# A hybrid Hyena and attention layer on one core: filter taps made with time on partitions, and the bias added by a DMA

## The chip, the cores and the metric

The kernel runs on one core of a Trainium2 chip. The metric is the device time of one execution in microseconds (us). Before the change the median of three runs is 2493.93 us (2493.28 to 2494.87). The core has TensorE (PE, matmuls; PEld are its weight loads), VectorE (DVE), ScalarE (ACT), GpSimd (POOL) and SyncE (SP), each with an instruction queue of its own that runs in order, and 16 DMA engines.

## The reference

One encoder layer on x of 1 x 512 x 2048, all in float32. The part that the change touches is the Hyena branch (1024 channels): a long two-sided filter for each channel, made by a small network from positions, is applied by FFT to z, and a bias per channel times z is added.

```python
def implicit_filter(L, w1, b1, w2, b2, w3, b3, w4, freq):
    ...
    h = jnp.sin(fr * (h @ w3.astype(f32) + b3.astype(f32)))
    h = h @ w4.astype(f32)
    ...
    decay = jnp.exp(-t[:, None] * deltas[None, :])
    h_fwd = h[:, :HYENA_W] * decay
    h_bwd = h[:, HYENA_W:] * decay
    k = jnp.concatenate([h_fwd, jnp.zeros((1, HYENA_W), f32), h_bwd[:0:-1]], axis=0)
    return k / jnp.sum(jnp.abs(k), axis=0, keepdims=True)

def hybrid_layer(x, ...):
    proj = rms_norm(x, mix_norm_g) @ w_in
    u_h, q, k, v, g = jnp.split(proj, [c0, c1, c2, c3], axis=-1)
    x0, x1, hv = jnp.split(centred_short_conv(u_h, hy_conv_w, hy_conv_b), HYENA_ORDER + 1, axis=-1)
    filt = implicit_filter(S, ...)
    z = hv * x1
    z = bidir_fft_conv(z, filt) + hy_bias * z
    y_h = z * x0
    ...                                    # attention on q, k, v gives y_a
    merged = g_h * (y_h @ w_br_hyena) + g_a * (y_a @ w_br_attn)
    x = x + merged @ w_out
    ...                                    # then a SwiGLU feed-forward
```

## The kernel before, in words

Activations lie with channels on partitions and the 512 tokens along the row; a tile is 128 x 512. Every product in full precision is split: a float32 operand becomes a rounded high part and a low rest (`split`: a cast on ScalarE, a subtraction on VectorE), and `mm3` multiplies high by high, high by low and low by high. Weights come as tiles of eight 128 x 128 blocks (`wblk`, lines 180 to 198): one DMA on SyncE, one cast `wh` on ScalarE, one subtraction `wl` on VectorE, three buffers each.

The main stream of TensorE is a row of column groups (`group`): the inputs x1, hv and x0 of the Hyena branch in order of channel tiles (`px`, `phv`), the keys and values (`kv`), the queries (`q`) and gates, and so on. After every block, three matmuls, it calls `step()`. A queue of Python generators runs behind `step()`: each `yield n` puts the rest of that work n steps later. So TensorE's order is written out by the program, and the numbers in `TURN_WAIT`, `Y_WAIT` and the yields are distances in steps. A scheduler places the other engines' work around it when the program is built. `flush()` behind `kv` runs what is left.

The Hyena channels are worked in four quarters q of two tiles c. For each quarter:

- `taps_gen(q)` (line 372): the last filter layer. For each tile, two products `fp` of 128 channels by 512 positions, forward and backward half, with the columns of `w4s` as weights and the hidden activations `hh` and `hl` as moving data; times the decay `dec` (lines 381 to 387). ScalarE sums |taps| along the row (`scr`, lines 391, 392), VectorE turns that into the norm `rn`, adds norm times bias to the tap at zero (line 395), and folds the two halves into sum `hs` and difference `hd` (lines 403 to 406).
- `filter_gen(q)` (line 411): sixteen 128 x 128 transposes `ktp` in two groups of eight bring time onto partitions (lines 417 to 422); ScalarE and VectorE turn them by cos and sin (`kt`, lines 426, 427) and split them. `TURN_WAIT` steps later come the spectrum products `kp`, VectorE makes `G` and `K` of them, and GpSimd stores `K` to DRAM (`kd`).
- `conv_gen(q)` (line 467): transposes of the folded input (`ztp`), eight steps on the products `up`, times the spectrum read back (`kc`), giving `Y`; then `taps_gen(q + 1)`, and `Y_WAIT` steps later the inverse products `ab`, scaled by `rn` into `abs_`; last the `y` rows (lines 533 to 543), multiplied by the gate input x0.

Work tiles of the filter come from the tag `wk` with seven buffers, scratch from `tmp` with five.

Of the kernel before, what the change touches and what calls it, by code (L numbers as in the profile page):

```python
# [118 lines left out]
def layer_kernel(tc, wpk, xT, par, flt, zemb, w4, decT, tb2, rope, qkg, out):  # L119
# [251 lines left out]

    def taps_gen(q):

        w4s = w4t.pop(q)
        rn, hs_l, hd_l = [], [], []
        for c in range(2):
            dec = cw(f"dec{q}{c}", [P, S], "dec", 1)
            nc.scalar.dma_start(dec, decT[2 * q + c])
            fd = work(f"fd{q}{c}")
            bd = cw(f"bd{q}{c}", [P, S + 1], "bd", 1)  # L380
            for half, dst in ((0, fd), (1, bd[:, :S])):
                fp = ps_tile(f"fp{q}{c}{half}")
                csl = slice(half * 256 + c * P, half * 256 + (c + 1) * P)
                mm(fp, w4s[:, csl], mlp["h"][0], True, False)
                mm(fp, w4s[:, csl], mlp["h"][1], False, True)
                nc.vector.tensor_tensor(dst, fp, dec, ALU.mult)
                yield 2
            nc.vector.memset(bd[:, S:S + 1], 0.0)
            n2 = cw(f"n2{q}{c}", [P, 2], "n2", 3)
            scr = tmp(f"scr{q}{c}")  # L390
            nc.scalar.activation(scr, fd, AF.Abs, accum_out=n2[:, 0:1])
            nc.scalar.activation(scr, bd[:, 1:], AF.Abs, accum_out=n2[:, 1:2])
            r = cw(f"rn{q}{c}", [P, 1], "rn", 4)
            nc.vector.tensor_tensor(r, n2[:, 0:1], n2[:, 1:2], ALU.add)
            nc.vector.scalar_tensor_tensor(fd[:, :1], r, pcol("hyb", 2 * q + c), fd[:, :1], ALU.mult, ALU.add)
            nc.vector.tensor_scalar(r, r, 256.0, None, ALU.mult)
            nc.vector.reciprocal(r, r)
            rn.append(r)

            hs, hd = work(f"hs{q}{c}"), work(f"hd{q}{c}")  # L400
            ahead = fd.rearrange("p (m n) -> p n m", n=2)
            back = bd[:, 1:].rearrange("p (m n) -> p n m", n=2)[:, ::-1]
            for h, op in ((hs, ALU.add), (hd, ALU.subtract)):
                h = h.rearrange("p (n m) -> p n m", n=2)
                nc.vector.tensor_tensor(h[:, :, :P], ahead[:, :, :P], back[:, :, :P], op)
                nc.vector.tensor_tensor(h[:, :, P:][:, :, ::-1], ahead[:, :, P:], back[:, :, P:], op)
            hs_l.append(hs)
            hd_l.append(hd)
        folded[q] = rn, hs_l, hd_l

    def filter_gen(q):
        rn, hs_l, hd_l = folded.pop(q)
# [3 lines left out]
        taps = []  # L416
        for i, src in enumerate((hs_l, hd_l)):
# [5 lines left out]
            with tc.high_priority():  # L423
                for j in range(2):
                    t = tmp(f"kt{q}{i}{j}")
                    nc.scalar.activation(t, tps[1 - j], AF.Copy, scale=pcol("sina" if i == j else "nsina"))
                    nc.vector.scalar_tensor_tensor(t, tps[j], pcol("cosa"), t, ALU.mult, ALU.add)
                    taps.append(split(cv, t, "kh", "kl", 4, 4, f"k{i}{q}{j}"))
            yield 3
# [1095 lines left out]
```

## Time and profile before

| | |
|---|---|
| median of 3 runs | 2493.93 us |
| profiled execution | 2493.58 us, its span 2491.8 us |
| stretch of the Hyena branch and the keys | about 60 to 375 us |
| transposes `ktp` | 64, between 89.1 and 312 us |
| tap products `fp` | 32, between 66.1 and 287 us |
| spectrum products `kp` | eight groups of six, between 100 and 326 us |
| last inverse products `ab` | end at 371 us |
| granted TensorE clock in all stretches | 1.00 |

How to read the rows. A row of a list of groups gives line, engine, operation, output and inputs by the program's names, shape and count; then the time that the group was busy, the mean ns of one, and the idle time of the engine just before them with what ended it. A row of a timeline gives start and length in us; several instructions of one kind are merged (x8). A row of one tile's instructions gives durations as min/median/max in ns. A row of waits gives the engine that waited, what it waited for, us in total, how often, and the longest. TensorE's durations overlap, since its matmuls are pipelined: the next one starts before the last one ends.

### The profile page before, as it was taken

How to read it: one execution, taken by the hardware profiler on the slowest of the kernel's cores; microseconds unless marked ns; L12 is line 12 of the kernel's file. 1: busy time of each engine (PE TensorE's matmuls, PEld its weight loads, DVE VectorE, ACT ScalarE, POOL GpSimd, SP SyncE). 2: the span in 40 equal slices, each digit the busy share in tenths (PEclk: the TensorE clock that was granted, in tenths of full speed). 3: DMA queues.
4: the chain of work that ended last, by engine and by line, in shares of the span. 5: the costliest groups of instructions: out<-in, count | busy, mean ns of one | idle time of the engine just before them, and what ended most of it. 6: DMA issues, size and time to landing. Idle time of an engine off the chain costs nothing.

```text
span 2491.8 us, 34447 instructions
## 1 busy us (share of the span) xinstructions
PE 2485.5 (100%) x13114; PEld 2140.8 (86%) x13114; DVE 2089.3 (84%) x2972; ACT 1191.4 (48%) x1778; POOL 185.0 (7%) x297
## 2 busy tenths in 40 slices
PE   9999999999999999999999999999999999999999
PEld 7888888888888888888888888888888888888888
DVE  8899986764589999555999989999999988998888
ACT  6444334654554455443544444444444455445443
POOL 0000113020000000000000000000000002001111
PEclk9999999999999999999999999999999999999999
DMA  6434443233554444644333333333333348557754
GB/s 216 132 123 131 140 144 113 70 102 119 185 177 157 148 141 152 194 163 136 121 125 117 127 117 120 127 120 127 118 119 125 121 144 221 146 146 187 193 152 110
DMA packets 113571, 350.48 MB, mean 141 GB/s; under 512 B 13987, under 2 KB 15267, under 8 KB 113181
## 3 DMA queue, kind: packets, MB, share of 16 engines
q1 hardware_dynamic: 70128, 248.02, 30.2%
q0 software_dynamic: 22832, 63.19, 9.6%
q10 hardware_dynamic: 20445, 37.07, 4.9%
q8 instruction: 103, 1.69, 0.3%
q14 instruction: 63, 0.52, 0.1%
HBM read 297.63 MB, written 54.26 MB: 141 GB/s over the span
## 4 chain that ended last, share of the span: by engine, by line
PE 96%; DVE 2%; DMA 1%; issue 0%; ACT 0%; ACTq 0%; SPq 0%; DVEq 0%; POOLq 0%
PE fx L137 19%; PE fy L137 10%; PE b L137 7%; PE o L137 7%; PE gx L137 7%; PE px L137 6%; PE d L137 5%; PE fz L137 5%; PE dx L137 4%; PE q L137 4%; PE ex L137 3%; PE gy L137 3%; PE phv L137 2%; PE ey L137 2%; PE dy L137 2%; PE kv L137 2%
## 5 line engine op out<-in xcount | busy, mean ns | idle before, releaser
L195 DVE TENSOR_TENSOR wl<-wr,wh 128x1024 fp32r<-128x1024 f32 (+1 forms) x168 | 201.2, 1198 | 110.8 <-ACT wh L194 110.6
L194 ACT CAST wh<-wr 128x1024 fp32r<-128x1024 f32 (+1 forms) x168 | 173.3, 1032 | 236.6 <-PE o L137 67.1
L919 ACT CAST fwhs<-fs 128x1024 fp32r<-128x1024 f32 x176 | 184.8, 1050 | 88.7 <-PE fz L137 73.6
L921 DVE TENSOR_TENSOR fwls<-fs,fwhs 128x1024 fp32r<-128x1024 f32 x176 | 214.3, 1218 | 4.3 <-ACT fwhs L919 4.2
L919 ACT CAST fwha<-fa 128x1024 fp32r<-128x1024 f32 x132 | 139.0, 1054 | 149.4 <-PE fx L137 83.4
L137 PE MATMUL px<-xh,wh 128*128 128x512 f32 x576 | 179.4, 393 | 0.4 <-ACT xh L559 0.3
L137 PE MATMUL fy<-fX,fwhs 128*128 128x512 f32 x704 | 175.4, 391 | 0.0
L137 PE MATMUL fx<-fX,fwhs 128*128 128x512 f32 x704 | 175.2, 391 | 0.0
L137 PE MATMUL fx<-fX,fwha 128*128 128x512 f32 x704 | 171.8, 391 | 0.0
L921 DVE TENSOR_TENSOR fwla<-fa,fwha 128x1024 fp32r<-128x1024 f32 x132 | 161.3, 1222 | 10.0 <-ACT fwha L919 9.9
L137 PE MATMUL o<-ms,wh 128*128 128x512 f32 x512 | 157.7, 389 | 0.0
L137 PEld LDWEIGHTS fx<-fX,fwha 128*128 128x128 f32 x704 | 129.3, 188 | 25.0
L137 PEld LDWEIGHTS fx<-fX,fwhs 128*128 128x128 f32 x704 | 129.2, 188 | 25.1
L137 PEld LDWEIGHTS fy<-fX,fwhs 128*128 128x128 f32 x704 | 129.2, 188 | 24.9
L137 PEld LDWEIGHTS px<-xh,wh 128*128 128x128 f32 x576 | 106.7, 188 | 23.3 <-issue 0.7
L137 PE MATMUL d<-act,wh 128*128 128x512 f32 x384 | 118.2, 389 | 0.0
L137 PEld LDWEIGHTS o<-ms,wh 128*128 128x128 f32 x512 | 96.0, 188 | 19.8
L137 PE MATMUL px<-xh,wl 128*128 128x512 f32 x288 | 112.5, 391 | 0.0
L912 DVE TENSOR_TENSOR fs<-fa,fa 128x1024 f32<-128x1024 f32 x88 | 107.0, 1217 | 1.7 <-PE o L137 1.0
L912 DVE TENSOR_TENSOR fs<-fs,fa 128x1024 f32<-128x1024 f32 x88 | 107.2, 1218 | 0.9 <-PE o L137 0.2
L137 PE MATMUL o<-ms,wl 128*128 128x512 f32 x256 | 99.6, 389 | 0.0
L137 PE MATMUL fy<-fX,fwls 128*128 128x256 f32 x704 | 98.7, 283 | 0.2 <-DVE fwls L921 0.2
(979 smaller groups left out, 5883.0 us busy)
## 6 DMA issues: line engine op xcount, KB each, us to landing
fa<-wpk SPq DMA_DIRECT2D x176, 512.0 KB, 3.6
wr<-wpk SPq DMA_DIRECT2D x162, 512.0 KB, 3.5
ga<-wpk SPq DMA_DIRECT2D x60, 512.0 KB, 3.7
da<-wpk SPq DMA_DIRECT2D x32, 512.0 KB, 3.7
ea<-wpk SPq DMA_DIRECT2D x32, 512.0 KB, 4.4
actd<-c POOLq DMA_DIRECT2D x41, 256.0 KB, 4.2
actr<-actd ACTq DMA_DIRECT2D x41, 256.0 KB, 5.1
x2d<-dt POOLq DMA_DIRECT2D x32, 256.0 KB, 5.7
```

What stands on the lines that cost most here:

```text
L137: tc.keep_in_program_order(nc.tensor.matmul(out, lhsT=lhsT, rhs=rhs, start=start, stop=stop, **kw))
L194: casts[i] = nc.scalar.copy(st["hi"][:, c], st["raw"][:, c]).ins
L195: nc.vector.tensor_tensor(st["lo"][:, c], st["raw"][:, c], st["hi"][:, c].bitcast(F32), ALU.subtract)
L912: raws["sum"] = nc.vector.tensor_tensor(t, a, b, ALU.add).ins
L919: raws["wh"] = nc.scalar.copy(hi, w).ins
L921: raws["wl"] = nc.vector.tensor_tensor(lo, w, hi.bitcast(F32), ALU.subtract).ins
```

## The change

The hidden activations become the weights of the tap products and the columns of `w4s` the moving data, so that the taps come out with time on partitions. The positions are put in an order (`zemb`) in which each product gives the even or odd taps of one half, forwards or backwards; `hh` gets two columns more for the taps past the end, and the decay table `decP` is laid out to fit. Each product group is four matmuls of 256 columns, and no transpose follows. The fold is one add and one subtraction on whole tiles. `turn_taps` does the turning by cos and sin right behind the products of the next quarter, in its own place of the queue.

The norm is a sum over partitions now: ScalarE takes |taps|, GpSimd adds the four tiles up (`fn`) and halves the row (`fo`), and two products `nr` with a column of ones, behind `ztp` (`norm_taps`), give it per channel. The bias no longer goes into the tap at zero: ScalarE scales the folded input by half the bias (`zh`), GpSimd's queue stores it to DRAM (`zd`), and a DMA adds it to `abs_`; in the last quarter it is read back (`zr`) and VectorE adds it. The `y` rows of a quarter are made behind the first half of the next quarter's spectrum (`y_rows`).

```diff
-TURN_WAIT = 8, 8, 10, 11
+TURN_WAIT = 11, 10, 11, 11
+UP_WAIT = 11, 12, 13, 13
...
-                hh, hl = cw("hh", [P, S], "hh", dt=F32R), cw("hl", [P, S], "hl", dt=F32R)
-                nc.scalar.copy(hh, a)
-                nc.vector.tensor_tensor(hl, a, hh.bitcast(F32), ALU.subtract)
+                hh, hl = (cw(n, [P, S + 2], n, dt=F32R) for n in ("hh", "hl"))
+                for o, src in ((slice(0, 385), a[:, :385]), (slice(386, 513), a[:, 385:]),
+                               (slice(385, 514, P), a[:, P:P + 1].to_broadcast([P, 2]))):
+                    nc.scalar.copy(hh[:, o], src)
+                    nc.vector.tensor_tensor(hl[:, o], src, hh[:, o].bitcast(F32), ALU.subtract)
...
+    TAPS = ((0, 129), (386, 257)), ((1, 129), (385, 257))
     def taps_gen(q):
         w4s = w4t.pop(q)
-        for c in range(2):
-            dec = cw(f"dec{q}{c}", [P, S], "dec", 1)
-            nc.scalar.dma_start(dec, decT[2 * q + c])
...
+        for j in range(2):
+            fb = []
+            for b in range(2):
+                dec = cw(f"dec{q}{j}{b}", [P, S], "dec", 2)
+                nc.scalar.dma_start(dec, decP[4 * q + 2 * j + b])
+                fp = ps_tile(f"fp{q}{j}{b}")
+                for n in range(2):
+                    a = TAPS[b][j][n]
+                    for i in range(2):
+                        mm(fp[:, n * 256:(n + 1) * 256], mlp["h"][i][:, a:a + P], w4s[:, b * 256:(b + 1) * 256],
+                           n == 0 and i == 0, n == 1 and i == 1, skip_group_check=True)
+                f = work(f"f{q}{j}{b}")
+                nc.vector.tensor_tensor(f, fp, dec, ALU.mult)
+                if j + b:
+                    t = tmp(f"fa{q}{j}{b}")
+                    nc.scalar.activation(t, f, AF.Abs)
+                    nc.gpsimd.tensor_tensor(acc, acc, t, ALU.add)
+                else:
+                    acc = work(f"fn{q}")
+                    nc.scalar.activation(acc, f, AF.Abs)
+                fb.append(f)
+                if not b:
+                    yield 2
+            f, b = fb
+            hs = work(f"hs{q}{j}")
+            nc.vector.tensor_tensor(hs, f, b, ALU.add)
+            nc.vector.tensor_tensor(f, f, b, ALU.subtract)
+            folded[q].append((hs, f))
+            yield 2
+        norms[q] = cw(f"fo{q}", [P, 256], "fo", 1)
+        nc.gpsimd.tensor_tensor(norms[q], acc[:, :256], acc[:, 256:], ALU.add)
+
+    def norm_taps(q):
+        acc = norms.pop(q)
+        nr = ps_tile(f"nr{q}")
...
+            mm(nr[:, c:c + 1], acc[:, c * P:(c + 1) * P], pcol("one"), True, True)
+        r = cw(f"rn{q}", [P, 2], "rn", 2)
+        nc.vector.tensor_scalar(r, nr[:, :2], 256.0, None, ALU.mult)
+        nc.vector.reciprocal(r, r)
+    def turn_taps(q):
+        taps = turned[q] = []
+        for i, tps in enumerate(zip(*folded.pop(q))):
+            for j in range(2):
+                t = tmp(f"kt{q}{i}{j}")
+                nc.scalar.activation(t, tps[1 - j], AF.Copy, scale=pcol("sina" if i == j else "nsina"))
+                nc.vector.scalar_tensor_tensor(t, tps[j], pcol("cosa"), t, ALU.mult, ALU.add)
+                taps.append(split(cv, t, "kh", "kl", 4, 4, f"k{i}{q}{j}"))
     def filter_gen(q):
...
-            tps = [ps_tile(f"ktp{q}{i}{j}") for j in range(2)]
-            for j, tp in enumerate(tps):
-                for n in range(4):
-                    o = n // 2 * 256 + j * P
-                    transpose(tp[:, n * P:(n + 1) * P], src[n % 2][:, o:o + P])
...
+            if q and i == 0:
+                y_rows(q - 1, sums.pop(q - 1))
     def conv_gen(q):
...
-        yield 8
+        norm_taps(q)
+        yield UP_WAIT[q]
...
             yield from taps_gen(q + 1)
-        yield Y_WAIT[q]
+            yield 5
+            turn_taps(q + 1)
+            yield Y_WAIT[q] - 5
+        else:
+            yield Y_WAIT[q]
...
+            if ph and q == NQ - 1:
+                zr = [tmp(f"zr{c}") for c in range(2)]
+                for c in range(2):
+                    nc.scalar.dma_start(zr[c], zd[c])
...
+        if q < NQ - 1:
+            for c in range(2):
+                nc.gpsimd.dma_start(abs_[c], zd[c], accum_op=ALU.add)
+            yield 1
+            sums[q] = abs_
+            return
         yield 1
+        for c in range(2):
+            nc.vector.tensor_tensor(abs_[c], abs_[c], zr[c], ALU.add)
+        y_rows(q, abs_)
...
     queue(taps_gen(0))
-    queue(pause(18))
+    queue(pause(11))
+    queue(turn_gen())
     queue(filter_gen(0))
...
-            zl.append(z)
+            zl.append(dpool.tile([P, S], F32, tag=f"zd{ct}", bufs=1, name=f"zd{ct}"))
+            zh = tmp(f"zh{ct}")
+            nc.scalar.activation(zh, zf, AF.Copy, scale=hybh[:, ct:ct + 1])
+            nc.gpsimd.dma_start(zl[c], zh)
```

What the change moves in the queues, at three places. Names carry the quarter and tile as digits and a buffer number behind the underscore; `wl13` is the low part of weight tile 13.

TensorE in quarter 0, where the first taps were transposed: before, eight `ktp` stand between two blocks of `phv2`, and eight more four blocks later.

```order
L137 MATMUL phv2_892<-xh0_127,wl14_895 128x512
L140 MATMUL ktp000_902<-ident_83,hs00_746 128x128
L140 MATMUL ktp000_902<-ident_83,hs01_792 128x128
L140 MATMUL ktp000_902<-ident_83,hs00_746 128x128
L140 MATMUL ktp000_902<-ident_83,hs01_792 128x128
L140 MATMUL ktp001_903<-ident_83,hs00_746 128x128
L140 MATMUL ktp001_903<-ident_83,hs01_792 128x128
L140 MATMUL ktp001_903<-ident_83,hs00_746 128x128
L140 MATMUL ktp001_903<-ident_83,hs01_792 128x128
L137 MATMUL phv2_892<-xh1_148,wh14_894 128x512 x2
```

In the changed program no such group exists; TensorE's only new place is behind the transposes of the input, which stand in both (here its end, with the norm's two products).

```order
L141 MATMUL ztp01_1106<-ident_83,zf0_679 128x128
L141 MATMUL ztp01_1106<-ident_83,zf1_700 128x128
L138 MATMUL nr0_1115<-prm_78,fo0_809 128x1 x2
L138 MATMUL px13_1041<-xh7_325,wh16_1043 128x512 x2
L138 MATMUL px13_1041<-xh7_325,wl16_1044 128x512
```

Gone are the sixteen transposes of a quarter; the norm's pair is what TensorE gets instead.

VectorE in quarter 0, ahead of the weight part `wl13`; before:

```order
L598 SCALAR_TENSOR_TENSOR hvo1_682<-hv1u_683,prm_78,hvo1_682 128x511
L597 SCALAR_TENSOR_TENSOR yh0_693<-x00u_694,prm_78,yh0_693 128x511
L617 TENSOR_TENSOR z1_688<-hvo1_682,x1o1_676 128x512
L598 SCALAR_TENSOR_TENSOR yh0_693<-x00u_694,prm_78,yh0_693 128x511
L621 TENSOR_TENSOR zf1_690<-z1_688 128x256 x2
L386 TENSOR_TENSOR bd00_715<-fp001_726,dec00_712 128x512
L195 TENSOR_TENSOR wl13_855<-wr13_853,wh13_854 128x1024
```

And now:

```order
L394 TENSOR_TENSOR f010_771<-fp010_766,dec010_764 128x512
L634 SCALAR_TENSOR_TENSOR x1o1_686<-x11u_687,prm_78,x1o1_686 128x511
L634 SCALAR_TENSOR_TENSOR hvo1_692<-hv1u_693,prm_78,hvo1_692 128x511
L635 SCALAR_TENSOR_TENSOR x1o1_686<-x11u_687,prm_78,x1o1_686 128x511
L635 SCALAR_TENSOR_TENSOR hvo1_692<-hv1u_693,prm_78,hvo1_692 128x511
L394 TENSOR_TENSOR f011_789<-fp011_784,dec011_782 128x512
L654 TENSOR_TENSOR z1_698<-hvo1_692,x1o1_686 128x512
L407 TENSOR_TENSOR hs01_794<-f010_771,f011_789 128x512
L658 TENSOR_TENSOR zf1_700<-z1_698 128x256 x2
L196 TENSOR_TENSOR wl13_896<-wr13_894,wh13_895 128x1024
```

All four products of the quarter (`f`) and three of the four fold operations stand ahead of `wl13` now, where two products stood before; the eviction `x00u` and the two multiplies on `yh0` have gone behind it.

VectorE at the end of the branch, from the last scaling of `ab` on; before:

```order
L531 SCALAR_TENSOR_TENSOR abs7_3436<-ab311_3474,rn31_2783,abl311_3497 128x2x128
L538 TENSOR_TENSOR y6_3500<-abs6_3435 128x2x128
L539 TENSOR_TENSOR y6_3500<-abs6_3435 128x2x128
L538 TENSOR_TENSOR y7_3504<-abs7_3436 128x2x128
L195 TENSOR_TENSOR wl58_3695<-wr58_3693,wh58_3694 128x1024
L543 TENSOR_TENSOR yh6_2936<-yh6_2936,y6_3500 128x512
```

And now:

```order
L551 SCALAR_TENSOR_TENSOR abs7_3417<-ab311_3455,rn3_3159,abl311_3485 128x2x128
L560 TENSOR_TENSOR abs6_3416<-abs6_3416,zr0_3472 128x512
L560 TENSOR_TENSOR abs7_3417<-abs7_3417,zr1_3473 128x512
L570 TENSOR_TENSOR y6_3490<-abs6_3416 128x2x128
L196 TENSOR_TENSOR wl58_3685<-wr58_3683,wh58_3684 128x1024
L571 TENSOR_TENSOR y6_3490<-abs6_3416 128x2x128
```

Two adds of the bias have come in ahead of the last `y` rows.

More of the change, by code (lines that the diff above doesn't have):

```diff
@@ L116, in weight_blocks, with layer_kernel @@
     return out
-def layer_kernel(tc, wpk, xT, par, flt, zemb, w4, decT, tb2, rope, qkg, out):
+def layer_kernel(tc, wpk, xT, par, flt, zemb, w4, decP, tb2, rope, qkg, out):
     nc = tc.nc
@@ L354, in mlp_gen @@
                 yield 6
-    filt, kd, folded = {}, {}, {}
+    kd, folded = {}, {}
     w4t = {}
@@ L370, in w4_parts @@
         w4t[q] = w4s
+    TAPS = ((0, 129), (386, 257)), ((1, 129), (385, 257))
+    norms, rns, sums, turned = {}, {}, {}, {}
     def taps_gen(q):
         w4s = w4t.pop(q)
-        rn, hs_l, hd_l = [], [], []
-        for c in range(2):
-            dec = cw(f"dec{q}{c}", [P, S], "dec", 1)
-            nc.scalar.dma_start(dec, decT[2 * q + c])
[L379 to L408, printed above, removed]
@@ L409, in taps_gen @@
-        folded[q] = rn, hs_l, hd_l
+        folded[q] = []
+        for j in range(2):
[27 more added lines that the diff above has]
+            yield 2
@@ new lines, in taps_gen @@
+        norms[q] = cw(f"fo{q}", [P, 256], "fo", 1)
[3 more added lines that the diff above has]
+        nr = ps_tile(f"nr{q}")
+        for c in range(2):
+            mm(nr[:, c:c + 1], acc[:, c * P:(c + 1) * P], pcol("one"), True, True)
+        r = cw(f"rn{q}", [P, 2], "rn", 2)
+        nc.vector.tensor_scalar(r, nr[:, :2], 256.0, None, ALU.mult)
+        nc.vector.reciprocal(r, r)
+        rns[q] = [r[:, c:c + 1] for c in range(2)]
@@ L411, in filter_gen @@
+    def turn_taps(q):
[6 more added lines that the diff above has]
+                taps.append(split(cv, t, "kh", "kl", 4, 4, f"k{i}{q}{j}"))
     def filter_gen(q):
-        rn, hs_l, hd_l = folded.pop(q)
@@ L415, in filter_gen @@
         yield 3
-        taps = []
-        for i, src in enumerate((hs_l, hd_l)):
-            tps = [ps_tile(f"ktp{q}{i}{j}") for j in range(2)]
-            for j, tp in enumerate(tps):
-                for n in range(4):
-                    o = n // 2 * 256 + j * P
-                    transpose(tp[:, n * P:(n + 1) * P], src[n % 2][:, o:o + P])
[L423 to L429, printed above, removed]
+        taps = turned.pop(q)
         if q + 1 < NQ:
@@ L539, in conv_gen, with turn_gen @@
             nc.vector.tensor_tensor(down[:, :, ::-1], a, b, ALU.subtract)
-            while ct not in x0st:
-                yield 1
             yh[ct] = x0st[ct]
             nc.vector.tensor_tensor(yh[ct], yh[ct], y, ALU.mult)
+    def turn_gen():
+        turn_taps(0)
+        yield 6
+    hybh = cw("hybh", [P, HT], "hybh")
+    nc.vector.tensor_scalar(hybh, prm[:, PC["hyb"]:PC["hyb"] + HT], 0.5, None, ALU.mult)
     xps = [ps_tile(f"px{i}") for i in range(XW)]
@@ L615, in layer_kernel @@
             hv = short_conv(p2, 16 + ct, f"hv{ct}", cw(f"hvo{ct}", [P, S], "sc", 3))
-            z = cw(f"z{ct}", [P, S], "z", 3)
+            z = cw(f"z{ct}", [P, S], "z", 2)
             nc.vector.tensor_tensor(z, hv, x1, ALU.mult)
@@ L1439, in _constants @@
     ang = (f4(2.0 * math.pi) * pos / f4(S))[:, None] * fb[None, :]
-    zemb = two_part(np.ascontiguousarray(np.concatenate([t[:, None], np.cos(ang), -np.sin(ang)], axis=-1).T, dtype=f4)).reshape(66, S)
+    zemb = two_part(np.ascontiguousarray(np.concatenate([t[:, None], np.cos(ang), -np.sin(ang)], axis=-1).T, dtype=f4))
+    order = np.concatenate([i[:257:2], i[1:256:2], i[511:256:-2], i[510:257:-2]])
+    zemb = zemb.reshape(66, S)[:, order]
     lo_d, hi_d = math.log(1e-2) / 1.5, math.log(1e-2) / 0.3
@@ L1443, in _constants @@
     dec = np.exp(-t[:, None] * deltas[None, :]).astype(f4)
-    decT = dec.T.reshape(HT, P, S)
+    p = i[:P]
+    n = np.arange(2)[:, None]
+    at = np.stack([[2 * p + n, 2 * p + 2 - n], [510 - 2 * p + n, 512 - 2 * p - n]])
+    decP = np.concatenate([dec, np.zeros((1, HW), f4)])[at].reshape(4, 2, P, NQ, 256)
+    decP = decP.transpose(3, 0, 2, 1, 4).reshape(4 * NQ, P, S)
     inv = np.power(f4(10000.0), -np.arange(0, 64, 2, dtype=f4) / f4(64)).astype(f4)
@@ L1454, in _constants @@
             rope[:, j, :, b:b + 64] = v.reshape(NTB, P, 64).transpose(1, 0, 2)
-    return tb2, cosw, sinw, cosa, sina, zemb, decT, rope
+    return tb2, cosw, sinw, cosa, sina, zemb, decP, rope
 def _arrays(inp):
@@ L1461, in _arrays @@
     assert all(v.dtype == f4 for v in a.values())
-    tb2, cosw, sinw, cosa, sina, zemb, decT, rope = _constants()
+    tb2, cosw, sinw, cosa, sina, zemb, decP, rope = _constants()
     blocks = weight_blocks()
```

8 lines of the change are left out of this document (4 added, 4 removed).

## The prediction

> **What bounds the kernel now.** I read the page's busy shares first, then TensorE's waits, then the stretch that the change touches (60 to 375 us) by engine.
>
> ```profile
> PE 2485.5 (100%) x13114; PEld 2140.8 (86%) x13114; DVE 2089.3 (84%) x2972; ACT 1191.4 (48%) x1778; POOL 185.0 (7%) x297
> PE warm L137 <- DVE wones L252: 1.1, 1, 1.1
> PE kp L137 <- DVE k121l L216: 0.5, 1, 0.5
> PE px L137 <- ACT xh L559: 0.3, 1, 0.3
> PE fy L137 <- DVE fwls L921: 0.2, 1, 0.2
> 60.00:375.00 315.00, 314.52 (x1497) 262.54 (x1496) 285.66 (x465) 133.09 (x204) 28.95 (x48) 1.00 0.42 134
> ```
>
> The four middle rows are all waits of TensorE in the whole program. In the last row (busy time of PE, PEld, DVE, ACT, POOL, then granted clock) TensorE has 0.48 us of idle time, VectorE 29.3 us. So TensorE's instruction stream sets the time, and a removed matmul is worth its issue interval, as long as nothing new makes TensorE wait. A matmul's listed duration overlaps the next one's, so I price by the distance of starts.
>
> **The transposes of the taps** go: eight groups of eight.
>
> ```profile
> L140 PE MATMUL ktp<-ident,hs 128*128 128x128 f32 x32 | 4.1, 272 | 0.0
> L140 PE MATMUL ktp<-ident,hd 128*128 128x128 f32 x32 | 4.1, 272 | 0.0
> 88.15 0.39 PE L137 MATMUL px<-xh,wh 128*128 128x512 f32 x1
> 88.38 0.39 PE L137 MATMUL px<-xh,wl 128*128 128x512 f32 x1
> 88.61 0.62 PE L137 MATMUL phv<-xh,wh 128*128 128x512 f32 x2
> ...
> 89.29 1.03 PE L140 MATMUL ktp<-ident,hs 128*128 128x128 f32 x8
> 90.08 0.71 PE L137 MATMUL phv<-xh,wh 128*128 128x512 f32 x2
> 90.62 0.40 PE L137 MATMUL phv<-xh,wl 128*128 128x512 f32 x1
> ```
>
> A 512-column matmul starts 0.23 us after the one before (88.15, 88.38, 88.61). From 89.29 to 90.62 there are eight transposes and two such matmuls: 1.33 - 0.46 = **0.87 to 0.88 us** for a group; the first matmul behind it is some 0.09 late, and that goes too. Eight groups: **-7.0 us**.
>
> **The tap products** change operands. Each of 16 groups was two 512-column matmuls and becomes four of 256 columns.
>
> ```profile
> 66.29 0.39 PE L137 MATMUL fp<-hh,w4s 128*128 128x512 f32 x1
> 66.52 0.39 PE L137 MATMUL fp<-hl,w4s 128*128 128x512 f32 x1
> 66.75 0.63 PE L137 MATMUL px<-xh,wh 128*128 128x512 f32 x2
> 1227.94 1.12 PE L137 MATMUL fy<-fX,fwls 128*128 128x256 f32 x8
> 1228.90 2.00 PE L137 MATMUL fy<-fX,fwhs 128*128 128x512 f32 x8
> ```
>
> A group took 0.46 us (66.29 to 66.75). Eight 256-column matmuls, each with its own weights, take 0.96 us (1227.94 to 1228.90), 0.12 each, so the new group takes 0.48: 16 x 0.02 = **+0.3 us**. Were each as long as its listed 0.283 us mean duration, it would be +10 us; the starts rule that out.
>
> **The column sums** `nr` are new: two 128x1 fp32 products in each quarter, behind transposes that stand there anyway. The nearest row is the token norm, four calls that the trace shows as eight instructions.
>
> ```profile
> 57.67 0.95 PE L137 MATMUL rs1ss<-prm,acc 128*128 128x1 f32 x8
> 58.48 0.71 PE L137 MATMUL px<-xh,wh 128*128 128x512 f32 x2
> ```
>
> That is 0.81 us, 0.10 an instruction. Two calls are four instructions, 0.41 us; four quarters: **+1.65 us**. Ends: 0.8 if a call is one instruction, 1.8 if each group pays the 0.09 again.
>
> **The wait at `kp`** should go.
>
> ```profile
> 250.39 0.40 PE L137 MATMUL kp<-k121h,CS 128*128 128x512 f32 x1
> 251.26 0.49 PE L137 MATMUL kp<-k121l,CS 128*128 128x512 f32 x1 [0.47 <-DVE k121l L216]
> 251.59 0.39 PE L137 MATMUL kp<-k121h,CS 128*128 128x512 f32 x1
> ```
>
> The 0.87 + 0.33 us between these starts are two intervals of 0.23 otherwise: **-0.75 us**. Today the taps are transposed 14 steps ahead of the `kp` that reads them, a step being three matmuls, 0.69 us. In the new program they are turned 22 steps ahead in quarter 0 and 29 in the others (15 to 20 us). What is late next is the products' own inputs, below.
>
> Sum: -7.0 + 0.3 + 1.65 - 0.75 = **-5.8 us**. The profiled execution took 2493.58 us (its span of 2491.8 and 1.8 around it), so 2487.8; the median of the runs shown is 0.35 above it, so **2488.1**.
>
> **What is hidden, and by what.** VectorE folds with 16 adds of 512 columns instead of 32 of 256, and drops 32 one-column operations.
>
> ```profile
> L406 DVE TENSOR_TENSOR hs<-fd,bd x8: 399/419/427, 80.8 to 304.6; 128x256 f32<-128x256 f32 x8
> L395 DVE SCALAR_TENSOR_TENSOR fd<-rn,prm,fd x8: 208/219/220, 81.1 to 305.2; 128x1 f32<-128x1 f32 x8
> L617 DVE TENSOR_TENSOR z<-hvo,x1o x8: 678/682/693, 71.3 to 308.7; 128x512 f32<-128x512 f32 x8
> ```
>
> By durations 32 x 0.42 against 16 x 0.68 is -2.5 us, the small operations up to -5, the two `zr` adds and four pairs on `rn` +2.6: VectorE's own work falls by 2 to 5 us. The turn's multiplies and casts (`kt`, `kh`, `kl`) stay as many, with SBUF sources instead of PSUM. ScalarE gains eight `zh` (0.7 us each, as `kt` is) and ten DMA issues (0.33), loses 16 accumulator reads (0.19): about +6 of its 182 idle us. GpSimd gains 14 DMAs (0.6 each) and 16 adds, in 286 idle us. All this costs nothing while TensorE's operands are ready in time.
>
> The new waits have work to hide them. `nr` waits for GpSimd's half add, and all of TensorE stands behind it; but it comes 47 steps (32 us) after the last product. On ScalarE `zh` waits for `zf`, and issues of `dec` wait for the product that frees their buffer, with weight casts behind them; ScalarE is idle for over half of the stretch. On GpSimd the bias DMA waits for `abs`; behind it stand the `kd` stores, due 15 steps later.
>
> Two places have little cover.
>
> The first is the weight split `wl13` in quarter 0. The order shows it behind five more 512-column operations, with `x00u` and two `yh` multiplies moved behind it.
>
> ```profile
> 78.97 0.68 DVE L386 TENSOR_TENSOR bd<-fp,dec 128x512 f32<-128x512 f32 x1
> 79.57 1.21 DVE L195 TENSOR_TENSOR wl<-wr,wh 128x1024 fp32r<-128x1024 f32 x1
> 83.62 0.39 PE L137 MATMUL px<-xh,wl 128*128 128x512 f32 x1
> ```
>
> At 0.60 us from start to start (78.97 to 79.57) and 0.66 a multiply, it is 5 x 0.60 - 0.60 - 2 x 0.66 = 1.1 us later. It ended at 80.78, wanted at 83.62: cover 2.84, so 1.7 us are left. ScalarE makes the first summand for GpSimd only behind `zf1`, so the first add falls behind or upon this split.
>
> The second is the end: `zr` puts two adds (1.2 us) ahead of the last `y`, and the key's tables load behind those.
>
> ```profile
> 392.07 0.42 DVE L709 TENSOR_TENSOR ko<-ko,kt 128x256 f32<-128x256 f32 x1
> 393.00 0.60 PE L140 MATMUL kT0p<-ident,ko 128*128 128x128 f32 x4
> ```
>
> Cover there is 0.5 us. But the last inverse products stand one step (0.69 us) earlier, so the `y` rows end about 0.5 us later, and GpSimd idled 1.4 us between `rpk` and `ko`. I take 0, up to 1 us. Everywhere else the split of weights had 5 us or more, and `kp`, `ztp` and with them the loads of `kc` come earlier. The bias DMA of a quarter lands some 15 steps ahead of the `y` rows that read it; DMA is at 0.42 of its time and gets some 6 MB more.
>
> **Rivals.**
>
> **Cover eaten in places** (a wait for VectorE in place of the one at `kp`). GpSimd's adds hold up VectorE.
>
> ```profile
> 44.23 1.36 POOL L344 TENSOR_TENSOR hs<-ha,hs 64x512 fp32r<-64x512 f32 x1 [1.99 <-ACT ha L343]
> 44.35 1.78 DVE L560 SCALAR_TENSOR_TENSOR xh<-xr,prm,xh 128x512 fp32r<-128x512 f32 x1
> 31.10 0.74 DVE L560 SCALAR_TENSOR_TENSOR xh<-xr,prm,xh 128x512 fp32r<-128x512 f32 x1
> ```
>
> The same multiply takes 1.78 us begun inside such an add and 0.74 alone: 1.04 lost. Three adds in a quarter lose up to 3.1 us, 1.4 more than the 1.7 left at `wl13` if all fell ahead of it; with 1 us at the end and the like elsewhere, 1 to 4 us come back: **2489 to 2492**. For it: VectorE is busy 91% of the stretch. Against it: covers of 5 us and more elsewhere.
>
> **GpSimd's adds make VectorE the bound** (the other side). The 12 adds and four half adds are 14 adds' worth. On 128 partitions an add has only these rows:
>
> ```profile
> L675 POOL TENSOR_TENSOR rpk<-rpk,gaink x8: 447/452/1439, 381.3 to 384.3; 128x128 f32<-128x128 f32 x8
> ```
>
> 512 columns are four of those: 1.8 us. If VectorE stands still through each, it loses 14 x 1.8 = 25 us. It has 29.3 idle and gains some 3, but 17 of the idle time are waits for `kc` (10.8) and for casts (6.1):
>
> ```profile
> L498 DVE TENSOR_TENSOR cu<-up,kc 128x1024 f32<-128x1024 f32 x16 | 19.5, 1219 | 10.8 <-DMA kc<-kd 10.8
> L195 DVE TENSOR_TENSOR wl<-wr,wh 128x1024 fp32r<-128x1024 f32 x47 | 57.3, 1218 | 6.1 <-ACT wh L194 6.1
> ```
>
> Then 285.7 - 3 + 25 + 17 = 325 us of VectorE stand against 315 - 6 = 309 of TensorE: 16 us more, **2504**. It decides from about 0.7 us lost per add (10 us in all); that the `kc` wait shrinks, since `kp` is earlier, and that adds meet operations with PSUM sources speak against it. The Trainium skill, page "SBUF — State Buffer", section "SBUF: two separate sides", says that VectorE and GpSimd share one port pair as an exclusive lock and that the other one "fully blocks"; the trace agrees (1.78 against 0.74), and by that rule every add that meets a two-input operation costs its whole rest.
>
> **The change does not do what it says**: 256-column products with `hh` as weights at 0.19 us, an LDWEIGHTS' duration, instead of 0.12 would cost 64 x 0.07 = 4.5 us and give 2492.6. The `fwls` rows have a fresh weight load each at 0.12, so I hold this unlikely.
>
> **How the numbers follow.** Clean sum: 0.60 (2487.5 to 2488.9). Cheap `nr`, 2487.2: 0.04. Cover eaten: 0.25. Products dearer: 0.03. VectorE the bound: 0.08. The range leaves out the last and the edges: 2487.0 to 2492.0. A measurement of this kernel tells 0.2% from no change, 5.0 us, so faster means below 2488.9: the first two cases, 0.64; eaten cover and dear products are within, 0.28; the rest slower, 0.08. The clean sum lies only 0.8 us beyond that bound.
>
> **What would show it.** No `ktp` group; `fp` groups 0.48 us from start to start; `nr` pairs 0.41; no TensorE wait at `kp`. Wrong would be: waits of TensorE for `wl` near 83 us, for `ko` near 387, or for `Yt` at `ab`; multiplies of VectorE of 1.5 us beside `fn` adds; VectorE over 95% busy in the stretch.

## The result, and the profile after

The changed kernel takes 2513.98 us (median of 4 runs, 2512.36 to 2514.43) where the kernel before took 2493.61 us beside it: ratio 1.0079, 95% interval 1.0066 to 1.0091. The prediction was 2488.1 us, 2492.0 at most. It is 20 us slower.

First the busy row of the changed kernel's page, then the window of the Hyena branch (columns as before: busy time of PE, PEld, DVE, ACT, POOL, then granted clock, DMA share, GB/s). Its span was 2512.3 us.

```profile
PE 2490.8 (99%) x13098; PEld 2142.9 (85%) x13098; DVE 2098.7 (84%) x2929; ACT 1195.1 (48%) x1772; POOL 219.7 (9%) x327
```

```profile
60.00:375.00 315.00, 301.21 (x1390) 248.83 (x1389) 275.43 (x393) 130.70 (x187) 62.87 (x78) 0.97 0.47 145
```

TensorE now has 13.8 us of idle time in the same 315 us (0.48 before), and VectorE, which was to lose 2 to 5 us of work, has 9.4 more in the whole program. The waits of TensorE in the changed kernel, longest in total first:

```profile
PE ab L138 <- DVE cu L509: 6.3, 1, 6.3
PE up L138 <- DVE zt20l L217: 2.0, 1, 2.0
PE ab L138 <- ACT Yt311h L216: 1.6, 1, 1.6
PE phv L138 <- DVE wl L196: 1.3, 1, 1.3
...
PE kv L138 <- DVE abs L551: 1.1, 1, 1.1
PE ab L138 <- DVE f L394: 0.9, 1, 0.9
```

No `kp` among them: that wait went, as the prediction had it. The largest one is in quarter 0. Around it, TensorE's timeline, and then the windows (the third number from the end is the granted clock):

```profile
149.61 0.39 PE L138 MATMUL px<-xh,wl 128*128 128x512 f32 x1
156.31 0.77 PE L138 MATMUL ab<-CS,Yt000h 128*128 128x256 f32 x2 [6.32 <-DVE cu L509]
...
160.46 1.16 PE L138 MATMUL px<-xh,wh 128*128 128x512 f32 x2
161.42 0.63 PE L138 MATMUL px<-xh,wl 128*128 128x512 f32 x1
```

```profile
140.00:149.60 9.60, 9.60 (x45) 8.00 (x45) 9.60 (x13) 2.81 (x5) 1.02 (x2) 1.00 0.55 155
149.60:156.30 6.70, 0.39 (x2) 0.02 (x1) 6.70 (x11) 1.96 (x3) 0.22 (x1) 0.80 0.42 144
156.30:163.90 7.60, 7.23 (x24) 6.28 (x25) 7.31 (x10) 1.86 (x3) 1.64 (x2) 0.50 0.34 107
```

The stall is paid twice: 6.5 us of standing, then 7.6 us at a granted clock of 0.50, worth another 3.8. VectorE was busy all through the stall (6.70 of 6.70). The clock falls a second time in quarter 2, behind the wait of `up` for `zt20l` (2.4 us between two starts, at 274.1), to 0.50 for some 7 us, worth up to 3.4:

```profile
278.70:283.00 4.30, 4.16 (x10) 3.29 (x11) 2.70 (x6) 0.81 (x1) 1.09 (x2) 0.50 0.78 263
```

Taken over 50 to 400 us, the starts of TensorE's matmuls lie 27.0 us further apart than the median of their shapes; before it was 2.2. Less the 5 us of work that TensorE no longer has, that is the 20 us.

Why VectorE was late shows first in ScalarE's timeline, 105 to 120 us, before and after:

```profile
105.01 0.59 ACT L441 COPY kc<-kp 128x512 f32<-128x512 f32 x1 [1.28 <-PE kp L137]
105.49 0.72 ACT L450 ACTIVATE kcr<-G,prm 128x512 f32<-128x512 f32 x1
```

```profile
103.10 0.59 ACT L451 COPY kc<-kp 128x512 f32<-128x512 f32 x1 [1.98 <-PE kp L138]
...
115.79 0.72 ACT L662 ACTIVATE zh<-zf,hybh 128x512 f32<-128x512 f32 x1 [3.19 <-DVE zf L658]
116.60 1.05 ACT L195 CAST wh<-wr 128x1024 fp32r<-128x1024 f32 x1
117.55 0.71 ACT L462 ACTIVATE kcr<-G,prm 128x512 f32<-128x512 f32 x1
```

`kcr`, ScalarE's part of `K`, had its inputs at 105.3, where the last `G` ended, and stands behind `zh` of the next quarter, which waits for `zf`. So it runs 12 us later than before, and with it `K`, the `kd` stores, the `kc` loads and `Y`. Second, VectorE's and GpSimd's timelines of the changed kernel in quarter 1, where a fold should take 0.68:

```profile
162.08 1.27 POOL L398 TENSOR_TENSOR fn<-fn,fa 128x512 f32<-128x512 f32 x1 [5.41 <-ACT fa L397]
165.31 3.38 POOL L398 TENSOR_TENSOR fn<-fn,fa 128x512 f32<-128x512 f32 x2 [1.96 <-ACT fa L397]
168.76 1.07 POOL L412 TENSOR_TENSOR fo<-fn 128x256 f32<-128x256 f32 x1
```

```profile
162.15 1.75 DVE L408 TENSOR_TENSOR f<-f,f 128x512 f32<-128x512 f32 x1
...
165.74 0.68 DVE L632 TENSOR_TENSOR x02u<-px,rbc 128x512 f32<-128x512 f32 x1
166.34 1.18 DVE L408 TENSOR_TENSOR f<-f,f 128x512 f32<-128x512 f32 x1
167.45 1.78 DVE L432 SCALAR_TENSOR_TENSOR kt<-hs,prm,kt 128x512 f32<-128x512 f32 x1
169.16 1.23 DVE L634 SCALAR_TENSOR_TENSOR yh<-x02u,prm,yh 128x511 f32<-128x511 f32 x1
```

Four operations of this quarter last 3.1 us longer than alone (1.07 + 0.50 + 1.04 + 0.49); `x02u`, which reads PSUM, takes its 0.68 inside an add. Over the four quarters it is 12.2 us, about half of it in the folds and 3.6 us in `kt`. Third, in quarters 1 to 3 the `y` rows stand between the two halves of the spectrum, and `kci` waits behind them (ScalarE's timeline, quarter 2):

```profile
263.34 0.72 ACT L462 ACTIVATE kcr<-G,prm 128x512 f32<-128x512 f32 x1 [1.07 <-DVE G L454]
263.97 1.04 ACT L195 CAST wh<-wr 128x1024 fp32r<-128x1024 f32 x1
268.24 0.72 ACT L463 ACTIVATE kci<-G,prm 128x512 f32<-128x512 f32 x1 [3.23 <-DVE G L454]
```

That gave three suspects: the **order** (`zh` ahead of `K`), GpSimd's **adds**, and the place of **y**.

### The profile page after: what moved, and what is told of

Same layout as the page of the kernel before. It is cut to its first block, busy times and chain, and to the rows that moved or that the text cites. A ratio compares the mean times of both kernels' runs of the same rounds, so it can differ in the third digit from the quotient of the medians.

```text
span 2512.3 us, 34460 instructions
## 1 busy us (share of the span) xinstructions
PE 2490.8 (99%) x13098; PEld 2142.9 (85%) x13098; DVE 2098.7 (84%) x2929; ACT 1195.1 (48%) x1772; POOL 219.7 (9%) x327
## 4 chain that ended last, share of the span: by engine, by line
PE 84%; DVE 1%; issue 0%; DMA 0%; ACT 0%; POOLq 0%; DVEq 0%; ACTq 0%
PE fx L138 19%; PE fy L138 10%; PE b L138 7%; PE o L138 7%; PE gx L138 7%; PE d L138 5%; PE fz L138 5%; PE dx L138 4%; PE q L138 3%; PE ex L138 3%; PE gy L138 3%; PE ey L138 2%; PE dy L138 2%; PE gz L138 2%; PE dz L138 1%; PE g L138 1%
## 5 line engine op out<-in xcount | busy, mean ns | idle before, releaser
L961 DVE TENSOR_TENSOR fwla<-fa,fwha 128x1024 fp32r<-128x1024 f32 x132 | 161.2, 1221 | 10.1 <-ACT fwha L959 10.0
```

What stands on the lines that cost most here:

```text
L961: raws["wl"] = nc.vector.tensor_tensor(lo, w, hi.bitcast(F32), ALU.subtract).ins
```

## The experiments

All are the changed kernel with the edits named, but for two that are the kernel before with something added. Times are medians; the ratio is to the kernel before, run beside them.

| run | us | ratio, 95% interval |
|---|---|---|
| changed kernel | 2514.0 | 1.0066 to 1.0091 |
| e1 bias over z | 2503.5 | 1.0025 to 1.0054 |
| e2 no bias | 2502.5 | 1.0023 to 1.0049 |
| e3 no adds | 2501.3 | 1.0021 to 1.0049 |
| e4 adds on VectorE | 2511.9 | 1.0060 to 1.0090 |
| e5 bias over z, no adds | 2493.4 | 0.9990 to 1.0008 |
| e6 bias over z, adds by DMA | 2512.6 | 1.0063 to 1.0088 |
| e7 as e6, y later | 2505.0 | 1.0032 to 1.0057 |
| e8 nr later | 2514.6 | 1.0069 to 1.0097 |
| e9 bias over z, y later | 2500.9 | 1.0015 to 1.0038 |
| e10 as e9, no adds | 2489.9 | 0.9976 to 0.9993 |
| e11 as e9, adds on VectorE | 2490.8 | 0.9978 to 0.9997 |
| e12 before, with GpSimd adds | 2503.9 | 1.0027 to 1.0052 |
| e13 before, with VectorE adds | 2502.3 | 1.0021 to 1.0042 |
| e14 as e9, adds of 16 columns | 2488.6 | 0.9965 to 0.9985 |
| e15 as e11, up later | 2491.8 | 0.9981 to 0.9999 |
| e16 bias over z, adds on VectorE | 2496.5 | 1.0003 to 1.0023 |

### The order

**e1**, the scaled bias written over `z`:

```diff
-            zh = tmp(f"zh{ct}")
-            nc.scalar.activation(zh, zf, AF.Copy, scale=hybh[:, ct:ct + 1])
-            nc.gpsimd.dma_start(zl[c], zh)
+            nc.scalar.activation(z, zf, AF.Copy, scale=hybh[:, ct:ct + 1])
+            nc.gpsimd.dma_start(zl[c], z)
```

> The changed kernel with one edit: ScalarE writes the scaled bias over z, which nothing reads any more, instead of taking one of the five tmp buffers. In the program's order the second quarter's first zh (zh2) then no longer stands ahead of kcr on ScalarE and z, zf no longer ahead of K on VectorE; all work stays. Order theory (zh2 takes its tmp buffer ahead of kcr, so K, the kd stores and the kc loads of quarter 0 start 12 us late): K back at about 106 to 113 us, no wait of TensorE of 6.3 us at ab in quarter 0 (149.6 us), and the fall of the granted clock behind it gone too: 2514 - 6 - 4 = 2504, or lower if the later quarters start with less backlog. Adds theory (GpSimd's adds hold VectorE up by 12 us, and that is the loss): the waits come elsewhere, 2510 to 2514.

Measured 2503.5, 10.5 us less, as the order theory had it. ScalarE's instructions in quarter 0 (some left out), in the changed kernel and then in e1:

```
COPY kc01<-kp010 128x512
CAST zt00h<-ztp00 128x512
ACTIVATE hvo2<-hv2u,prm 128x512
CAST zt01h<-ztp01 128x512
ACTIVATE zh2<-zf2,hybh 128x512
ACTIVATE kcr00<-G000,prm 128x512
```

```
COPY kc01<-kp010 128x512
ACTIVATE kcr00<-G000,prm 128x512
ACTIVATE kci00<-G001,prm 128x512
```

`zh` and `kcr` both draw from the five `tmp` buffers, and `zh2` comes first in the program; given another buffer for `zh`, the scheduler puts `kcr` first again. In e1's trace `kcr` runs at 107.66, not 117.55:

```profile
107.66 0.72 ACT L462 ACTIVATE kcr<-G,prm 128x512 f32<-128x512 f32 x1
```

The 6.3 us wait is gone; smaller ones came up (2.8 us for a weight split at 94 us), so half the loss stays.

**e2**, the bias left out (`zh`, `zd`, the DMA onto `abs_`, and `zr` in the last quarter):

```diff
-            nc.scalar.activation(zh, zf, AF.Copy, scale=hybh[:, ct:ct + 1])
-            nc.gpsimd.dma_start(zl[c], zh)
...
-                nc.gpsimd.dma_start(abs_[c], zd[c], accum_op=ALU.add)
...
-            nc.vector.tensor_tensor(abs_[c], abs_[c], zr[c], ALU.add)
```

> The changed kernel without the bias: no zh, no zd, no DMA added to abs, no zr adds; the filter taps as in the change, GpSimd's adds included. Order theory: quarter 0 as without zh2, and no wait for the bias DMA ahead of G in the other quarters: 2488 to 2500, most of the 20 us back. Adds theory: at least 12 of the 20 us stay, 2506 or more.

Measured 2502.5, between the two cases: 11.5 us less, no more than e1 within the spread of the runs. So of the bias it is the buffer that costs; its eight ScalarE operations and 14 DMAs on GpSimd's queue, kept in e1, cost about 1 us or nothing.

**e8**, the column sums behind the products `up` instead of ahead of them:

```diff
-        norm_taps(q)
         yield UP_WAIT[q]
...
                 yield 5
+        norm_taps(q)
         if q + 1 < NQ:
```

> The changed kernel with the column sums nr and the two operations on rn emitted behind the four spectra products of a quarter instead of behind ztp; nothing else. VectorE waited 3.5 us for nr in quarter 0 with zt00l, hvo and the weight split behind. If that wait is a cause of the loss: 2 to 4 us less than the changed kernel, 2510 to 2512. If K behind zh2 decides, the same chain ends as late: 2513 to 2515.

Measured 2514.6: nothing. VectorE's 3.5 us wait for `nr` was real, but `K` stood behind `zh2` anyway (`kcr` at 116.79).

### GpSimd's adds

**e3** leaves the adds out (the norm is then that of one tap tile's half):

```diff
-                    nc.gpsimd.tensor_tensor(acc, acc, t, ALU.add)
...
-        nc.gpsimd.tensor_tensor(norms[q], acc[:, :256], acc[:, 256:], ALU.add)
+        nc.scalar.copy(norms[q], acc[:, :256])
```

> The changed kernel without GpSimd's adds: the 12 adds of fa to fn are left out and fo is a ScalarE copy of half of fn, so the filter's norm is that of one of its tap tiles; everything else stays, K behind zh2 too. Adds theory: VectorE gets 12 us back (its operations beside the adds last 0.45 to 1.15 us longer than alone), so 2514 less 12 to 20: 2494 to 2502. Order theory: the late K of quarter 0 is kept, so its waits stay for the most part: 2506 to 2514.

Measured 2501.3: 12.7 us less, and the wait at `ab` in quarter 0 is still there (5.8 us). The time is as the adds theory had it, the kept wait as the order theory had it: neither was the whole. **e4** makes the adds on VectorE:

```diff
-                    nc.gpsimd.tensor_tensor(acc, acc, t, ALU.add)
+                    nc.vector.tensor_tensor(acc, acc, t, ALU.add)
...
-        nc.gpsimd.tensor_tensor(norms[q], acc[:, :256], acc[:, 256:], ALU.add)
+        nc.vector.tensor_tensor(norms[q], acc[:, :256], acc[:, 256:], ALU.add)
```

> The changed kernel with the 12 adds and 4 half adds on VectorE instead of GpSimd: VectorE pays 12 x 0.6 + 4 x 0.35 = 8.6 us of its own where the trace shows it losing 12.2 us beside GpSimd's adds. If only VectorE's time counts: 3 to 4 us less, 2510. If the lock between the two engines costs more than the time that the durations show: 2500 or less. Order theory: within 4 us of the changed kernel, 2510 to 2516.

Measured 2511.9, 2.1 us less: it decides nothing, since with `K` still behind `zh2` TensorE waits for VectorE at `ab` in quarter 0 all the same (5.4 us). **e12** puts the same load on the kernel before, where nothing else is wrong (and **e13** the same with `nc.vector`):

```diff
             nc.scalar.activation(scr, bd[:, 1:], AF.Abs, accum_out=n2[:, 1:2])
+            for _ in range(2):
+                nc.gpsimd.tensor_tensor(scr, scr, scr, ALU.add)
```

> The kernel before with 16 added GpSimd adds of 128x512 (two behind each tap tile's norm, doubling a scratch tile that nothing reads), four a quarter where the change has three and a half. Nothing else. Adds theory: VectorE's operations beside them last longer by some 12 us in all, of which its idle time in the stretch (29 us) hides a part; TensorE's waits and the lower clock behind them add up to 4 to 12 us: 2498 to 2506. If adds cost only a kernel that is already behind: 2493 to 2495.

Measured 2503.9, 10.3 us more, though VectorE's and ScalarE's instructions stand in the same order as before, one by one. Two rows of VectorE's timeline, in e12 beside an add begun at 80.33, and in the kernel before:

```profile
80.43 1.02 DVE L396 TENSOR_TENSOR rn<-n 128x1 f32<-128x1 f32 x1
81.70 0.99 DVE L397 SCALAR_TENSOR_TENSOR fd<-rn,prm,fd 128x1 f32<-128x1 f32 x1
```

```profile
80.70 0.15 DVE L394 TENSOR_TENSOR rn<-n 128x1 f32<-128x1 f32 x1
81.10 0.21 DVE L395 SCALAR_TENSOR_TENSOR fd<-rn,prm,fd 128x1 f32<-128x1 f32 x1
```

An operation on one column takes 1.0 us: it stands still until GpSimd is done. That is the lock of the Trainium skill, page "SBUF — State Buffer", section "SBUF: two separate sides", which the prediction named; here the trace agrees.

> The kernel before with the same 16 added adds of 128x512, on VectorE instead of GpSimd: 16 x 0.6 = 9.6 us of VectorE's own time, more than the 8.6 us by which GpSimd's adds stretched its operations (there the time rose by 10.3 us). If VectorE's lost time is what counts, whoever takes it: 2501 to 2506. If VectorE's own adds, which stand in its queue where the planner put them, are hidden better: 2494 to 2498.

Measured 2502.3, 8.4 us more. VectorE's busy time, 2089.3 us before, is 2097.1 in e13, 7.8 more, and 2102.6 in e12, 13.3 more (not 8.6, as the expectation had it: the one-column operations were missing there). So in the kernel before a microsecond taken from VectorE cost 0.8 (e12) to 1.1 us (e13), whoever took it, though VectorE has 29 us of idle time in the stretch: the idle time is not where it is needed. That is the price at one place. In both runs most of TensorE's waiting is for the fold ahead of the transposes, which the changed kernel no longer has (first e12, then e13):

```profile
PE ktp L140 <- DVE hs L407: 4.7, 3, 2.5
```

```profile
PE ktp L140 <- DVE hs L407: 5.8, 3, 3.2
```

**e14** keeps every add, buffer and wait of e9 (below), but adds 16 columns only (the half add too, on a ScalarE copy), so the norm leaves the other columns out:

```diff
-                    nc.gpsimd.tensor_tensor(acc, acc, t, ALU.add)
+                    nc.gpsimd.tensor_tensor(acc[:, :16], acc[:, :16], t[:, :16], ALU.add)
```

> The kernel with the scaled bias over z and y behind the second half (2500.9 with GpSimd's adds, 2489.9 without), with GpSimd's adds kept in number, place, buffers and waits but over 16 columns instead of 512 and 256 (so the norm is wrong but in those columns). If the time that GpSimd computes beside VectorE is the price: 2490 to 2492. If it is the chain of waits through GpSimd (fa and fn held until its adds are done): 2497 to 2501.

Measured 2488.6 against 2500.9 with full adds, and below the 2490 to 2492 expected. So it is the time that GpSimd computes, not the number of its operations and waits. That this time acts by holding VectorE up, and not by holding buffers longer, rests on the stretched rows above and on e12, whose adds nothing reads. The bias DMAs, the scaling of the folded input and their place in the queues are all in this run, so in this order none of these costs anything. Why it lies 1.3 us under e10, which has no adds but a 1.5 us wait for the weight split at 94 us, was not followed. It is also the only run without a wait of TensorE beyond the warm-up's; its answer to the question for waits, and the stretch, read:

```profile
PE warm L138 <- DVE wones L253: 1.1, 1, 1.1
```

```profile
60.00:375.00 315.00, 315.00 (x1505) 264.07 (x1504) 286.68 (x429) 141.01 (x214) 45.73 (x78) 1.00 0.51 157
```

### Both, and the place of y

**e5** is e1 and e3 together:

> Both edits that each gave half of the loss back: the scaled bias written over z, and GpSimd's adds left out (the norm is that of one tap tile). If the order and the adds are two causes that add up: 2514 - 10.5 - 12.7 = 2491 or a little less; the prediction's clean sum was 2488. If they are two names of one lack of VectorE's time, either edit is enough and together they give less than the sum: 2496 to 2500.

Measured 2493.4: the savings of 10.5 and 12.7 us add up to 23.2, and 20.6 came. Two causes, then, but 5 us above the clean sum. In **e7** and **e9** the `y` rows stand one place later:

```diff
-            if q and i == 0:
+            if q and i == 1:
                 y_rows(q - 1, sums.pop(q - 1))
```

> The whole computation, with GpSimd's adds: the scaled bias written over z (2503.5 alone), and the y rows emitted behind the second half of the next spectrum. With DMA adds this move of y was worth 7.6 us. If y between the halves holds up K whatever sums the norm: 2495 to 2499. If it only helped because the DMA adds had made the bias late: 2502 to 2504.

Measured 2500.9, 2.6 us less than e1: as the second case, or a little better. **e10**, the same without adds:

> The same without GpSimd's adds (the norm is that of one tap tile). All three suspects are away: zh2's buffer, the adds, y between the halves. If these are all the causes, the prediction's sum for TensorE holds: 2488 to 2490. If VectorE still is too full: 2492 to 2494, as with y between the halves (2493.4).

Measured 2489.9, 3.5 us less than e5, with no overlap of the runs (2489.51 to 2490.27 against 2492.57 to 2494.40). In e5 TensorE waited for PSUM tiles that VectorE's product `f` frees, at 222 to 228 us; in e10 it did not. TensorE's timeline of e5:

```profile
224.05 0.71 PE L138 MATMUL px<-xh,wh 128*128 128x512 f32 x2 [0.95 <-DVE f L394]
...
228.25 0.47 PE L138 MATMUL ab<-CS,Yt101h 128*128 128x256 f32 x2 [0.98 <-DVE f L394]
```

So `y` between the halves is a third, smaller cause. Part of it may be its wait for the bias DMA, once 0.95 us in the changed kernel, 2.8 in e1, 2.1 in e5 and none in e9 and e10. How it leads to these waits by way of `K` and `Y` was not followed step by step.

**e6** and **e7** do the adds by DMAs that add at their destination:

```diff
-                    nc.gpsimd.tensor_tensor(acc, acc, t, ALU.add)
+                    nc.gpsimd.dma_start(acc, t, accum_op=ALU.add)
...
-        nc.gpsimd.tensor_tensor(norms[q], acc[:, :256], acc[:, 256:], ALU.add)
+        nc.scalar.copy(norms[q], acc[:, :256])
+        nc.gpsimd.dma_start(norms[q], acc[:, 256:], accum_op=ALU.add)
```

> The whole computation: the scaled bias written over z, and the 12 adds and 4 half adds of the norm done by DMAs that add at their destination (16 more DMAs on GpSimd's queue, a ScalarE copy of 256 columns a quarter) in place of GpSimd's adds. If what hurts is GpSimd computing beside VectorE: VectorE's operations no longer stretch beside them and the time is that of the run without adds, within 2 us. If GpSimd's DMA issues hold VectorE up as its adds do, or the DMAs delay the kc loads: 2498 or more.

> The run with DMA adds, and the y rows of a quarter emitted behind the second spectrum half of the next instead of between the halves, so that kci on ScalarE and the second G on VectorE do not stand behind y and its wait for the bias DMA. If y between the halves delays K and with it what TensorE needs in quarters 1 to 3: 1 to 3 us below the run with DMA adds. If VectorE's total is what counts: within 1 us of it.

Measured 2512.6 and 2505.0. e6 is in its second case (2498 or more), but 19 us above e5, and not by the reasons given there: VectorE waited 18.0 us for the `kc` loads, hardly more than the 16.4 in e5. ScalarE's waits in e6 point to another:

```profile
ACT fo L412 <- DMA fn<-fa: 12.2, 4, 6.1
...
ACT kt L432 <- DMA fn<-fa: 7.7, 3, 3.2
```

Each `fa` holds one of the five `tmp` buffers until its DMA, chained behind the one before, has landed; `kt` needs that buffer. The same ring of buffers again, in place of the lock. That the buffers are the whole of it was not tried by itself. Putting y later gave back 7.6 us here, more than the 1 to 3 expected.

**e11** and **e16** take e1's edit and e4's adds on VectorE, e11 with y later as well:

> The whole computation: scaled bias over z, y behind the second half, the norm's adds on VectorE (8.6 us of its own time). If VectorE's time is the price in this stretch, it stands 3 to 9 us above the run without adds and 0 to 4 below the one with GpSimd's: 2493 to 2498.

> The whole computation: the scaled bias over z, the norm's adds on VectorE, y still between the halves of the next spectrum. With y behind the second half, VectorE's adds cost 0.9 us over no adds at all (2490.8 and 2489.9); with y between, no adds gave 2493.4 and GpSimd's adds 2503.5. If VectorE's own adds are cheap because they stand in its queue where the planner put them: 2494 to 2496. If that was luck of one order, and VectorE's 8.6 us cost what GpSimd's do: 2500 to 2503.

Measured 2490.8, below the 2493 to 2498 expected, and 2496.5, half a microsecond above its first case: VectorE's adds cost 0.9 and 3.1 us over no adds, GpSimd's 11.0 and 10.1. **e11 computes everything and is faster than both kernels**, 2.8 us under the kernel before (ratio 0.9978 to 0.9997). Why VectorE's own 7.4 us (2094.5 us busy in e11, 2087.1 in e10) are hidden here and not in e13 stays partly open. The scheduler lays out VectorE's adds with the rest (apart from the adds, many rows of VectorE's order differ between e10 and e11), and it left that order as it was when GpSimd's were added in e12; that this is the reason was not isolated.

**e15**, the last quarter's products `up` two steps later:

```diff
-UP_WAIT = 11, 12, 13, 13
+UP_WAIT = 11, 12, 13, 15
```

> The whole computation in the best order so far (scaled bias over z, y behind the second half, adds on VectorE: 2490.8), with the up products of the last quarter two steps later, since TensorE waited 0.85 us there for zt31l. If that wait was late by itself: 2490. If the two steps push what follows: 2491 to 2493.

Measured 2491.8. The wait at `up` went, and a wait of 1.7 us for `ko` at `kT0p` came, the place near 387 us whose cover of 0.5 us the prediction had counted.

## Why the prediction was wrong, point by point

- **TensorE's sum was right.** e14, in which nothing waits, took 2488.6 us, 2488.61 in its profiled execution, against 2487.8 by the sum. Its rows: four `fp` products in 0.47 us from start to start, as the 0.48 taken; one quarter's `nr` 0.36 where 0.41 was taken, and the matmul behind it 0.10 late, as `ktp`'s was:

```profile
69.92 0.28 PE L138 MATMUL fp<-w4s,hh 128*128 128x256 f32 x1
...
70.39 0.62 PE L138 MATMUL px<-xh,wh 128*128 128x512 f32 x2
...
107.97 0.50 PE L138 MATMUL nr<-prm,fo 128*128 128x1 f32 x4
108.33 0.72 PE L138 MATMUL px<-xh,wh 128*128 128x512 f32 x2
```

- **VectorE's own work fell** by 3.4 us (2085.9 in e14, 2089.3 before), inside the 2 to 5 predicted. In the changed kernel the adds took 12.2 back and more.
- **The step that failed** is "The new waits have work to hide them", and in it "On ScalarE `zh` waits for `zf` ... ScalarE is idle for over half of the stretch". An idle share hides nothing for what stands behind a waiting instruction. Weight casts were named as what is behind; the `kcr` that carries `K` was not, and the working shows no row of ScalarE's order. From it came the false sentence that "`kp`, `ztp` and with them the loads of `kc` come earlier": `kp` was, the loads were 10.5 us later in quarter 0, and VectorE's waits for them grew from 10.8 to 17.6 us. Price 8 to 10.5 us (e3 to e5, and e1).
- **The adds** were a rival at 0.08, 2504 us. Its mechanism, the lock, was right: e1 and e9, with the adds kept and the order mended, took 2503.5 and 2500.9. That 2504 lies so near is in part luck. It set 25 us lost by VectorE, and 12.2 were lost; with 12.2 its own sum gives 285.7 - 3 + 12.2 + 17 = 312 us of VectorE against 309 of TensorE, some 2491, while the adds cost 10.1 to 12.7 (e1 to e5, e9 to e10, e3). VectorE did not become the bound either: it was busy 275 of the 315 us, 87%. The time was lost at the few places where TensorE stood waiting for it. What was also wrong is the chance, and the weight given to adds that "meet operations with PSUM sources". Those are spared (`x02u` above), but the folds have SBUF sources, and the change itself gave them to the turn's multiplies: `kt` took 0.75 us on average before and 1.19 for the first half after. The case of eaten cover, 1 to 4 us, was too small by the same reading.
- **y** behind the bias DMA was taken as landing "some 15 steps ahead". It did not: `y` waited 0.95 us for it in quarter 2, with `G` and `kci` behind. The place of `y` as a whole cost 2.6 to 3.5 us (e1 to e9, e5 to e10).
- **The places with little cover**: no wait for `wl13` near 83 us and none for `ko`; the weight split that came late is the one at 94 us. Of the other signs of being wrong two came, `ab` waiting for `Yt` and multiplies of over 1.5 us beside `fn` adds; VectorE over 95% busy did not.

## What to carry to other kernels

A small engine's idle share is no cover: before an instruction that waits is added, list what stands behind it in its queue, and which ring of buffers it draws on, since a tile taken early in the program can push an urgent one behind it. An engine that is 90% busy beside a bound one has hardly any time to give; until a run shows better, price a microsecond taken from it as a microsecond (0.8 to 1.1 in e12 and e13, but 0.1 in e11), and GpSimd's SBUF work as work of VectorE's. When a change loses, mend its causes one at a time and together: here three of them hid a gain of 5 us, and half of it could be had.
